# A gMLP's output projection by seven block products instead of eight, with its last column group in another order and the next norm's sums of squares finished by token halves

## The chip, the cores and the metric

The kernel runs on one core of one Trainium2 chip. The metric is the device time of one execution in microseconds (us), as the median of the runs of a kernel. The core's engines appear in the profile as PE (TensorE, matmuls), PEld (its weight loads), DVE (VectorE), ACT (ScalarE), POOL (GpSimd) and SP (SyncE, which here only issues transfers). "SPq", "POOLq" and "ACTq" are the queues through which an engine issues its DMA transfers.

## The reference

The kernel computes a causal decoder trunk of two layers over 512 tokens and 1024 channels in float32. This case concerns the first half of layer 0:

```
def mixer_a(xn, w_in, g_v, w_s, b_s, w_out):
    z = jax.nn.gelu(xn @ w_in)
    u, v = jnp.split(z, 2, axis=-1)
    v = rmsnorm(v, g_v)
    ...
    s = jnp.einsum('hts,bcshd->bcthd', w, v) + b_s.T.astype(v.dtype)[None, None, :, :, None]
    s = s.reshape(B, S, A_WIDTH)
    return (u * s) @ w_out
```

Its result is added to the residual stream h. Then comes `conv_ffn(rmsnorm(h, norm_ffn), ...)`: an up projection to 2 x 2816 channels, a causal convolution of width 3, silu(g) * u, and a down projection that is added to h. Then a per-layer embedding is added, `(p_i @ w_in) * gate`, in which `p_i @ w_in` depends on no h. `rmsnorm` divides each token by the root of the mean of its 1024 squares.

## The kernel before, in words

**Layout.** h lies transposed, as eight tiles h[0] to h[7] of 128 channels by 512 tokens, so a matmul's moving operand has up to 512 columns of tokens. Float32 products are made of three: every operand is split into a high part (the cast `wh`, `ush`, `usl` and so on: a high part ends in h, a low part in l) and the rest, and `mm3` (matmuls at L228) multiplies high by high, high by low and low by high into one accumulator bank of PSUM. A projection from 1024 to 1024 channels is therefore eight output tiles of 8 x 3 = 24 matmuls of 512 columns, 192 in all.

**Weights.** All weights are a list of pieces in order of use (`plan_cols`, `plan_woven`, L63 to L128). SP loads each piece into one of three staging buffers (`load`, L166), ACT casts the high parts (L196), DVE subtracts to get the low parts (L197). A piece is split in units of up to 1024 columns; four units may be ahead of use (`WBUFS`). The instructions of an engine keep the order in which they are scheduled; `behind(x, y)` only says that x shall come after y.

**Seven block products.** The first two of three parts of the FFN's down projection already use `woven_add`. It takes a pair of contraction tiles, a pair of output tiles and the two token halves `first` and `second` as a 2 x 2 by 2 x 2 product of blocks and forms it with seven block multiplications instead of eight, at the price of sums: three sums of weight blocks per piece on DVE (`weave`, L156 to L158) and sums and differences of activations (class `Pair`, L468 to L480). A product is 4 pairs x 3 = 12 matmuls of 256 columns, so a group of 256 output channels takes 84, and the four groups 336. The numbers 1 to 7 name the products. Products 1, 6, 7 and 4 accumulate one after another in half a bank called `dx`; between them that half is copied out (L531, L537, L511), since the partial sums go to different outputs. Products 2, 5 and 3 go into the bank `dy`. The copies, `head`, `rest`, `side` and `tail`, are added to h by accumulating DMA transfers on POOL's queue (L508). Product 4 of a group is run in the next one (`close`), and in the last group product 7 comes before 3, in the others 3 before 7.

**The projection and its surroundings.** In the gating stage (L792 to L818) u is made in four chunks of two tiles: 48 matmuls, then for each tile the gelu and 8 small matmuls of the position mixing (L805), and DVE forms u * s and its splits. Then `dense_add` makes the output projection: after each tile's 24 matmuls (bank `d`) DVE adds the bank to h[m] (L445), ACT squares it (L331), and the squares are added up in `nf0acc` (L336), on POOL for all but the last, which DVE adds. Two small transposes (`turned`, L825) follow, and their copy by DVE (L826).

**The norm.** DVE transposes the sum in blocks of 32 and reduces them (L350, L352, `nf0quarter`); a small matmul `nf0ms` (L361) finishes the mean; DVE adds epsilon (`nf0m`, L426), POOL raises it to the power -1/2 (`nf0rt`, L428), DVE makes an operand of it (`nf0hl`, L381 and L382; `nf0d`, L390), and a matmul `nf0sp` (L394) spreads the factors over all partitions, so that DVE can scale h (L404) for the up projection. PE meanwhile does the embedding's input projection, eight banks of 6 matmuls `pin` (L628 on): `nf0ms` stands after the third bank and `nf0sp` after the sixth. After the eighth, `up` begins (L570).

Of the kernel before, what the change touches and what calls it, by code (L numbers as in the profile page):

```python
# [13 lines left out]
P = 128  # L14
D = 1024
S = 512
# [34 lines left out]
def tile_yoco(ctx: ExitStack, tc: tile.TileContext, t, out: bass.AP, out_b: bass.AP):  # L51
# [64 lines left out]
    plan_cols(t["w_out"], 4, KD)  # L116
# [17 lines left out]
    state = {"raw": 0, "unit": 0, "next": 0, "tags": [0, 1, 2], "turn": 4, "pt": 0, "sent": {}}  # L134
# [82 lines left out]
    def mm3(ps, parts, xs, c0, n=P, first=True, last=True, lows_last=False, onto=False):  # L217
# [9 lines left out]
        for j, (w, x) in enumerate(todo):  # L227
            nc.tensor.matmul(ps, w, x, start=first and j == 0, stop=last and j == len(todo) - 1,  # L228
                             skip_group_check=onto)
# [87 lines left out]
    class Norm:  # L317
# [22 lines left out]
        def take(self, k):  # L340
            if not self.late:
                self.split(k, 0)
            self.square(k, nc.vector if k == KD - 1 else None)
            if self.behind is not None:
                self.behind(k)

# [73 lines left out]
    def inv_root(ms, name, scale=1.0, n=None):  # L420
# [4 lines left out]
        for some, x in ms:  # L425
            nc.vector.tensor_scalar(m[some, :], x, scale, EPS, op0=ALU.mult, op1=ALU.add)  # L426
        r = const.tile([P, n], F32, tag=f"rt{n}", bufs=2, name=f"{name}rt")
        nc.gpsimd.tensor_tensor(r, m, minus_half[:, :n], op=ALU.pow)  # L428
        return r

# [28 lines left out]
    class Pair:  # L459


        def __init__(self, p, edge, name):
            self.p, self.name = p, name
            self.edge = edge[:, p, 0, :], edge[:, p, 1, :]

        def begin(self, a):
            self.a = a
            self.own, self.ones, self.twos = (couple(homes[3 * self.p + x], f"{self.name}_{x}") for x in range(3))  # L468
# [23 lines left out]
    def woven_add(pairs, between):  # L492
# [9 lines left out]
        def product(x, ps, w, at0, first=True):  # L502
            wh, wl = w[:2]
            mm3(ps, [(wh, wl, at0 + k * P) for k in range(len(pairs))], ops[x], 0, first=first,
                onto=not first)
# [7 lines left out]
        def close(c, chain, w, tail):  # L513
            def run():
                product(4, chain, w, 0, first=False)
                minus(tail[:, first], chain)
                onto(h[2 * c + 1], tail)
            return run

        late = None  # L520
        for c in range(4):
            top, low = h[2 * c], h[2 * c + 1]
            chain, other = psum(f"dx{c}")[:, first], psum(f"dy{c}")
            head = tp.tile([P, S], F32, tag="acc", name=f"head{c}")
            tail = tp.tile([P, S], F32, tag="sq", name=f"tail{c}")
            side = tp.tile([P, N], F32, tag="c1", name=f"side{c}")
            rest = tp.tile([P, S], F32, tag="c0", name=f"rest{c}")
            w = unit()
            product(1, chain, w, 0)
            product(2, other[:, first], w, n)  # L530
            nc.scalar.copy(head[:, first], chain)  # L531
            w = unit()
            product(5, other[:, second], w, n)
            product(6, chain, w, 0, first=False)
            minus(side, other[:, second])
            onto(low[:, second], side)
            nc.scalar.copy(head[:, second], chain)  # L537
            onto(top, head)
# [3 lines left out]
            for x in (7, 3) if c == 3 else (3, 7):  # L542
                if x == 3:
                    product(3, other[:, second], w, n, first=False)
                else:
                    product(7, chain, w, 0, first=False)
                    minus(tail[:, second], chain)
            nc.scalar.copy(rest, other)
            onto(top, rest)
            late = close(c, chain, unit(), tail)  # L550
            if c == 0:
                between()
# [848 lines left out]
```

## Time and profile before

Three runs took 1118.29, 1118.88 and 1119.21 us, a median of 1118.88. The profiled execution took 1118.13 us, with a span of 1116.3 us from its first to its last instruction.

| | before |
|---|---|
| gating stage, from its last chunk's matmuls to the projection | 87.57 to 100.25 us |
| output projection, 192 matmuls | 100.25 to 143.79 us |
| `nf0ms`, the norm's mean | 148.19 us |
| `nf0sp`, the norm's factors spread | 152.76 us |
| first matmuls of `up` in the chain | 155.78 us |
| a woven part of the FFN, 336 matmuls | 253.71 to 294.11 us |

All times inside an execution count from the start of the span. In a row of the chain the columns are the start, the duration and the work, with a count. In a row of a timeline they are the start, the duration from the first to the last of a run of like instructions, engine, line, operation and tiles, and in brackets how long the engine was idle before and what released it. In a row of the grouped view, line, engine, operation, tiles, shapes and count stand before the first bar; then the busy time in us and the mean of one in ns; then the idle time before. Tile names come without their numbers.

### The profile page before, as it was taken

How to read it: one execution, taken by the hardware profiler on the slowest of the kernel's cores; microseconds unless marked ns; L12 is line 12 of the kernel's file. 1: busy time of each engine (PE TensorE's matmuls, PEld its weight loads, DVE VectorE, ACT ScalarE, POOL GpSimd, SP SyncE). 2: the span in 40 equal slices, each digit the busy share in tenths (PEclk: the TensorE clock that was granted, in tenths of full speed). 3: DMA queues.
4: the chain of work that ended last, by engine and by line, in shares of the span. 5: the costliest groups of instructions: out<-in, count | busy, mean ns of one | idle time of the engine just before them, and what ended most of it. 6: DMA issues, size and time to landing. Idle time of an engine off the chain costs nothing.

```text
span 1116.3 us, 15052 instructions
## 1 busy us (share of the span) xinstructions
PE 1107.6 (99%) x5693; PEld 947.3 (85%) x5693; DVE 793.8 (71%) x1244; ACT 580.8 (52%) x968; POOL 158.0 (14%) x227
## 2 busy tenths in 40 slices
PE   9999999999999999999999999999999999999997
PEld 7888888889988898888888888888899889988886
DVE  5566368687477675567988997877784777655796
ACT  5733255445544464455656775554464545544543
POOL 1200210002200030012204452000022000300210
PEclk9999999999999999999999999999999999999999
DMA  8632334216931287233134225632179222971333
GB/s 295 137 114 95 113 114 151 76 38 153 244 114 41 84 195 258 84 114 113 54 98 132 77 57 178 213 118 76 38 174 235 101 73 55 226 250 57 114 100 90
DMA packets 46921, 140.95 MB, mean 126 GB/s; under 512 B 12984, under 2 KB 20672, under 8 KB 36352
## 3 DMA queue, kind: packets, MB, share of 16 engines
q1 hardware_dynamic: 35952, 120.38, 33.6%
q0 software_dynamic: 9328, 14.95, 7.6%
q10 hardware_dynamic: 1568, 4.65, 1.1%
q8 instruction: 45, 0.74, 0.3%
q14 instruction: 28, 0.23, 0.1%
HBM read 112.69 MB, written 6.30 MB: 107 GB/s over the span
## 4 chain that ended last, share of the span: by engine, by line
PE 96%; DVE 1%; issue 1%; ACT 1%; POOLq 0%; POOL 0%; DVEq 0%
PE up L228 41%; PE d L228 9%; PE dx L228 8%; PE dy L228 6%; PE o L228 4%; PE q L228 4%; PE gate L228 4%; PE u L228 4%; PE up L570 2%; PE pv L1093 1%; PE v L238 1%; PE v L239 1%; PE v L240 1%; PE pin L228 1%; PE k L228 1%
## 5 line engine op out<-in xcount | busy, mean ns | idle before, releaser
L197 DVE TENSOR_TENSOR wl<-wraw,wh 128x1024 fp32r<-128x1024 f32 (+2 forms) x198 | 232.4, 1179 | 169.6 <-ACT wh L196 168.6
L196 ACT CAST wh<-wraw 128x1024 fp32r<-128x1024 f32 (+2 forms) x197 | 193.7, 990 | 147.1 <-PE up L228 60.6
L582 DVE SCALAR_TENSOR_TENSOR c<-up,vec,c 128x510 f32<-128x510 f32 (+1 forms) x176 | 130.9, 747 | 31.6 <-ACT c L580 29.3
L228 PE MATMUL up<-nf00h,wh 128*128 128x512 f32 x336 | 130.7, 389 | 0.0
L228 PE MATMUL up<-nf10h,wh 128*128 128x512 f32 x336 | 130.7, 389 | 0.0
L228 PE MATMUL up<-nf00l,wh 128*128 128x512 f32 x336 | 130.7, 389 | 0.0
L228 PE MATMUL up<-nf10l,wh 128*128 128x512 f32 x336 | 130.7, 389 | 0.0
L228 PE MATMUL up<-nf10h,wl 128*128 128x512 f32 x336 | 130.5, 389 | 0.0
L228 PE MATMUL up<-nf00h,wl 128*128 128x512 f32 x336 | 130.4, 389 | 0.0
L580 ACT ACTIVATE c<-up,vec 128x512 f32<-128x512 f32 x88 | 68.1, 776 | 44.2 <-PE up L228 39.0
L228 PEld LDWEIGHTS up<-nf00h,wl 128*128 128x128 f32 x336 | 63.1, 188 | 13.2
L228 PEld LDWEIGHTS up<-nf10h,wh 128*128 128x128 f32 x336 | 63.1, 188 | 13.2
L228 PEld LDWEIGHTS up<-nf10h,wl 128*128 128x128 f32 x336 | 63.1, 188 | 13.1
L228 PEld LDWEIGHTS up<-nf00h,wh 128*128 128x128 f32 x336 | 63.1, 188 | 13.0
L228 PEld LDWEIGHTS up<-nf00l,wh 128*128 128x128 f32 x336 | 63.1, 188 | 13.0
L228 PEld LDWEIGHTS up<-nf10l,wh 128*128 128x128 f32 x336 | 63.1, 188 | 12.9
L508 POOL DMA_DIRECT2D h<-side x16 | 14.0, 874 | 403.8 <-ACT side L511 403.8
L197 DVE TENSOR_TENSOR wl<-wsum,wh 128x1024 fp32r<-128x1024 f32 x32 | 39.1, 1223 | 28.5 <-ACT wh L196 28.5
L588 ACT ACTIVATE a<-c 128x512 f32<-128x512 f32 x44 | 27.7, 630 | 39.9 <-DVE c L582 39.9
L196 ACT CAST wh<-wsum 128x1024 fp32r<-128x1024 f32 x32 | 33.6, 1051 | 18.4 <-PE up L228 10.0
L1037 ACT ACTIVATE prs<-prs,neg 128x129 f32<-128x129 f32 x64 | 25.3, 397 | 13.4 <-DVE neg L1032 12.5
L445 DVE TENSOR_TENSOR h<-h,d 128x512 f32<-128x512 f32 x24 | 16.4, 682 | 21.5 <-PE d L228 21.5
(537 smaller groups left out, 2702.7 us busy)
## 6 DMA issues: line engine op xcount, KB each, us to landing
wraw<-in_w_up SPq DMA_DIRECT2D x44, 1024.0 KB, 4.9
wraw<-in_w_down SPq DMA_DIRECT2D x16, 1024.0 KB, 4.9
wraw<-in_w_gate SPq DMA_DIRECT2D x8, 1024.0 KB, 5.0
wraw<-in_w_down SPq DMA_DIRECT2D x8, 768.0 KB, 4.2
wraw<-in_w_u SPq DMA_DIRECT2D x4, 1024.0 KB, 10.2
wraw<-in_w_out SPq DMA_DIRECT2D x4, 1024.0 KB, 4.8
h<-head POOLq DMA_DIRECT2D x16, 256.0 KB, 4.8
h<-rest POOLq DMA_DIRECT2D x16, 256.0 KB, 7.8
```

The lines of the kernel that those rows point to most:

```text
L196: cast = nc.scalar.copy(hi, src)
L197: state["split"] = splits[u] = cast, nc.vector.tensor_sub(low, src, hi.bitcast(F32))
L228: nc.tensor.matmul(ps, w, x, start=first and j == 0, stop=last and j == len(todo) - 1, skip_group_check=onto)
L238: nc.tensor.matmul(ps, xh[:, s], wh[:, a:b], start=st, stop=False)
L239: nc.tensor.matmul(ps, xl[:, s], wh[:, a:b], start=False, stop=False)
L445: nc.vector.tensor_add(h[m], h[m], ps)
L508: nc.gpsimd.dma_start(x, y, accum_op=ALU.add)
L570: nc.tensor.matmul(ps, w[:, off + s * P : off + (s + 1) * P], x, start=k == 0 and x is xh and w is wh, stop=k == KD - 1 and x is xl)
L580: nc.scalar.activation(c, ps, AF.Identity, bias=v("conv_b", l * 2 * NJ + col), scale=cw[2])
L582: ins = nc.vector.scalar_tensor_tensor(c[:, tap:], ps[:, : S - tap], cw[2 - tap], c[:, tap:], op0=ALU.mult, op1=ALU.add)
L588: nc.scalar.activation(a, cs[0], AF.Silu)
L1037: ins = nc.scalar.activation(pr[:, e, :], pr[:, e, :], AF.Exp, bias=neg[:, e : e + 1], scale=-1.0, accum_out=sm[:, e : e + 1])
```

## The change

The output projection's weights are planned as woven, four pieces of four units (1024, 1024, 1024 and 512 columns). The gating stage hands over four `Pair`s instead of eight split tiles; each chunk's two tiles are a pair. For the last chunk the order of the splits is different (`soon`): the difference of the token halves of its first tile is split at once, and its second tile's own split comes first of all. `dense_add` is replaced by `woven_add(us, norm=nf, ...)`, which differs from the FFN's use of it in these points:

- In the first group, products 1, 2 and 5 are run for three pairs, then for the last pair.
- The first two groups add to h by accumulating transfers, as in the FFN, but the last two by additions and subtractions on DVE (`direct`).
- The last group (`ends`) is written out: products 1 and 2, then 4 of the group before, 5, 6, 7, 4 and 3. The scheduler puts `turned` between 6 and 7, and three `pin` between 7 and 4. Fifteen `pin` follow before `nf0ms`, which stays behind the third bank.
- The squares of h[0] to h[5] are summed whole (four adds on POOL, the fifth on DVE). Those of h[6] and h[7] are added, transposed and reduced by token halves on DVE (`by_halves`).
- The copy `turned` and the splits of the first two units of `up` are placed behind `nf0m` on DVE, ahead of `nf0hl`.

In every norm, `take` now gives the last two adds of squares to DVE instead of the last one. In the FFN's woven parts the last group now runs product 3 before 7, as the other groups do.

```diff
-    plan_cols(t["w_out"], 4, KD)
+    plan_woven(t["w_out"], 4, 0, KD)
...
-    state = {"raw": 0, "unit": 0, "next": 0, "tags": [0, 1, 2], "turn": 4, "pt": 0, "sent": {}}
+    state = {"raw": 0, "unit": 0, "next": 0, "tags": [0, 1, 2], "turn": 6, "pt": 0, "sent": {}}
...
-            self.square(k, nc.vector if k == KD - 1 else None)
+            ins = self.square(k, eng or (nc.vector if k >= KD - 2 else None))
...
+        def by_halves(self):
+
+            sqs, a = {}, self.acc
+            sq = tp.tile([P, S], F32, tag="sg", name=f"{self.name}turn")
+            self.quarter = const.tile([P, S // 32], F32, tag="quarter", bufs=1, name=f"{self.name}quarter")
+
+            def add(k, cols):
+                if k not in sqs:
+                    sqs[k] = tp.tile([P, S], F32, tag="sq", name=f"{self.name}sq{k}")
+                ins = nc.scalar.activation(sqs[k][:, cols], h[k][:, cols], AF.Square)
+                return ins, nc.vector.tensor_add(a[:, cols], a[:, cols], sqs[k][:, cols])
+
+            def turn(cols):
+                ins = nc.vector.transpose(sq[:, cols], a[:, cols])
+                return ins, nc.vector.tensor_reduce(self.quarter[:, cols.start // 32 : cols.stop // 32],
+                                                    sq[:, cols].rearrange("p (b f) -> p b f", f=32),
+                                                    axis=mybir.AxisListType.X, op=ALU.add)
+            return add, turn
...
-        def begin(self, a):
+        def begin(self, a, soon=False):
...
+            if soon:
+                split(self.t[:, first], *(x[:, first] for x in self.ones))
...
-        def end(self, b):
+        def end(self, b, soon=False):
             t, u = self.t, tp.tile([P, S], F32, tag="sq", name=f"{self.name}u")
+            if soon:
+                split(b, *self.own)
...
+            if soon:
+                split(u, *self.twos)
+                split(t[:, second], *(x[:, second] for x in self.ones))
+                return
...
-    def woven_add(pairs, between):
+    def woven_add(pairs, between=None, norm=None, tags=("acc", "sq", "c1", "c0")):
...
+                if direct(c):
+                    nc.scalar.copy(tail[:, first], chain)
+                    nc.vector.tensor_sub(h[2 * c + 1], h[2 * c + 1], tail)
+                else:
+                    minus(tail[:, first], chain)
+                    onto(h[2 * c + 1], tail)
...
+        def direct(c):
+            return norm is not None and c > 1
...
+        def ends(c, top, low, chain, other, head, tail):
+
+            w = unit()
+            product(1, chain, w, 0)
+            product(2, other[:, first], w, n)
+            ins = nc.scalar.copy(head[:, first], chain)
+            for m in (2 * c - 2, 2 * c - 3):
+                ins = square(m, ins)
+            late()
+            square(2 * c - 1, None, nc.vector)
+            add, turn = norm.by_halves()
+            w = unit()
+            product(5, other[:, second], w, n)
+            product(6, chain, w, 0, first=False)
+            nc.vector.tensor_sub(low[:, second], low[:, second], other[:, second])
+            nc.vector.tensor_add(top[:, first], top[:, first], other[:, first])
+            nc.scalar.copy(head[:, second], chain)
+            nc.vector.tensor_add(top, top, head)
+            add(2 * c, first)
+            w = unit()
+            product(7, chain, w, 0, first=False)
+            nc.scalar.copy(tail[:, second], chain)
+            nc.vector.tensor_sub(low[:, second], low[:, second], tail[:, second])
+            add(2 * c + 1, second)
+            ends = product(4, chain, unit(), 0, first=False)
+            behind(product(3, other[:, second], w, n, first=False)[0], ends[-1])
+            nc.scalar.copy(tail[:, first], chain)
+            nc.vector.tensor_sub(low[:, first], low[:, first], tail[:, first])
+            seq = [add(2 * c + 1, first)[1]]
+            seq.append(nc.vector.tensor_add(top[:, second], top[:, second], other[:, second]))
+            seq += turn(first)
+            box["sq"], ins = add(2 * c, second)
+            seq += [ins, *turn(second)]
...
+            i = state["next"] + 2
+            behind(splits[i][0], box["sq"])
+            behind(splits[i][1], box["quarter"])
...
+            if c == 0 and norm is not None:
+                w2 = unit()
+                for some in (slice(-1), slice(-1, None)):
+                    product(1, chain, w, 0, first=some.stop is not None, some=some)
+                    if some.stop is None:
+                        nc.scalar.copy(head[:, first], chain)
+                    product(2, other[:, first], w, n, first=some.stop is not None, some=some)
+                    product(5, other[:, second], w2, n, first=False, some=some)
+                w = w2
...
-            for x in (7, 3) if c == 3 else (3, 7):
...
+            product(3, other[:, second], w, n, first=False)
+            product(7, chain, w, 0, first=False)
+            (nc.scalar.copy if direct(c) else minus)(tail[:, second], chain)
+            if direct(c):
+                nc.vector.tensor_add(top, top, head)
+                nc.vector.tensor_add(top, top, other)
+            else:
+                nc.scalar.copy(rest, other)
+                onto(top, rest)
...
+            if norm is not None and c > 1:
+                for m in range(2 * c - 1):
+                    square(m, mark)
...
                     if (c, q, j) == (0, 1, 0):
                         norm.begin(rows=0)
+                        behind(box.pop("turned"), box["m"])
+                        for i in (0, 1):
+                            cast, low = splits[state["next"] + i]
+                            behind(cast, box["sq"])
+                            behind(low, box["m" if i else "quarter"])
...
-            hi = ap.tile([P, S], F32R, tag=f"ah{m}", name=f"ush{m}")
-            lo = ap.tile([P, S], F32R, tag=f"al{m}", name=f"usl{m}")
-            split(u, hi, lo)
-            us.append((hi, lo))
+            (us[c].end if j else us[c].begin)(u, soon=c == 3)
     nf = Norm("nf0", [(xp, "x", gain("norm_ffn", 0))], late=True)
-    dense_add(us, KD, nf)
+    woven_add(us, norm=nf, tags=("c0", "c1", "hs", "sg"))
```

More of the change, by code (lines that the diff above doesn't have):

```diff
@@ L500, in unit, with product @@
             return take()
-        def product(x, ps, w, at0, first=True):
+        def product(x, ps, w, at0, first=True, some=slice(None)):
             wh, wl = w[:2]
-            mm3(ps, [(wh, wl, at0 + k * P) for k in range(len(pairs))], ops[x], 0, first=first,
-                onto=not first)
+            return mm3(ps, [(wh, wl, at0 + k * P) for k in range(len(pairs))][some], ops[x][some], 0,
+                       first=first, onto=not first)
         def onto(x, y):
@@ L541, in woven_add @@
                 late()
-            for x in (7, 3) if c == 3 else (3, 7):
[L543 to L549, printed above, removed]
+            product(3, other[:, second], w, n, first=False)
+            product(7, chain, w, 0, first=False)
+            (nc.scalar.copy if direct(c) else minus)(tail[:, second], chain)
+            if direct(c):
+                nc.vector.tensor_add(top, top, head)
+                nc.vector.tensor_add(top, top, other)
+            else:
+                nc.scalar.copy(rest, other)
+                onto(top, rest)
             late = close(c, chain, unit(), tail)
-            if c == 0:
+            if c == 0 and between:
                 between()
+            if norm is not None and c > 1:
+                for m in range(2 * c - 1):
+                    square(m, mark)
         late()
```

66 lines of the change are left out of this document (39 added, 27 removed).

## The prediction

> **What bounds the kernel now.** I read the page first, then the chain that ended last in order of time around the output projection, then the grouped rows of the stage that already works as the projection is to work, and last the timelines of the engines at the projection's two ends.
>
> ```profile
> span 1116.3 us, 15052 instructions
> PE 1107.6 (99%) x5693; PEld 947.3 (85%) x5693; DVE 793.8 (71%) x1244; ACT 580.8 (52%) x968; POOL 158.0 (14%) x227
> ...
> PE 96%; DVE 1%; issue 1%; ACT 1%; POOLq 0%; POOL 0%; DVEq 0%
> ```
>
> TensorE (PE) carries 96% of the chain. A matmul fewer is worth its pitch, and any wait that reaches PE costs its full length.
>
> ```profile
> 100.25 43.53 PE d L228 x192
> 143.79 0.22 PE turned L825 x2
> 144.01 4.19 PE pin L228 x18
> 148.19 0.29 PE nf0ms L361 x2
> 148.49 4.28 PE pin L228 x18
> 152.76 0.23 PE nf0sp L394
> ```
>
> The projection is 192 matmuls of 512 columns with no gap, 43.53/192 = 0.2267 us each. The norm after it is hidden under `pin`, work that needs no norm: 18 `pin` before `nf0ms`, 18 before `nf0sp`.
>
> ```profile
> 253.71 1.40 PE dx L228 x12
> ...
> 291.23 1.44 PE dy L228 x12
> 292.67 1.44 PE dx L228 x12
> 294.11 5.92 PE up L228 x26
> ```
>
> These are the first and last rows of the chain of an FFN down projection already done with seven block products: four groups of 7 x 12 = 336 matmuls of 256 columns, from 253.71 to 294.11, 40.40 us or 0.1202 us each. The chain names no wait between them.
>
> **The change, part by part.** *Arithmetic.* 192 matmuls of 512 columns become 336 of 256. By the two stretches that is 43.53 - 40.40 = 3.13 us less. The FFN's stretch also has the same weight sums and the same accumulating transfers beside it, so I take -3.13, and it is the ceiling of the gain: all that follows only takes from it. On the pitch the row stands at 0.120 us. [...]
>
> *Weight sums and operand splits.* Four pieces of weights are summed on VectorE (DVE), and each gets four splits instead of two, one of them half as long.
>
> ```profile
> L156 DVE TENSOR_TENSOR wsum<-wraw 128x1024 f32<-128x1024 f32 x8 | 9.8, 1220 | 0.1
> L157 DVE TENSOR_TENSOR wsum<-wsum,wraw 128x512 f32<-128x512 f32 x8 | 5.5, 688 | 0.2
> ...
> L480 DVE SCALAR_TENSOR_TENSOR act_0u<-act_0u,a 128x256 f32<-128x256 f32 x2 | 0.8, 420 | 0.0
> ...
> L531 ACT COPY head<-dx 128x256 f32<-128x256 f32 x8 | 3.0, 373 | 3.1 <-PE dx L228 3.1
> ...
> 60.00:98.50 38.50, 38.50 (x196) 32.77 (x196) 23.91 (x31) 14.70 (x20) 0.00 (x0) 1.00 0.24 83
> ...
> 100.00:143.80 43.80, 43.80 (x198) 36.18 (x196) 18.92 (x22) 14.11 (x18) 8.99 (x6) 1.00 0.32 108
> ...
> 253.60:294.20 40.60, 40.60 (x339) 40.45 (x338) 27.68 (x31) 24.67 (x42) 12.22 (x14) 1.00 0.80 194
> ```
>
> A sum is 1.22 and twice 0.69 (its third operation has the second's form), 2.6 us per piece. The last three rows are windows (sum, then busy PE, weight load, DVE, ACT, POOL): the projection has DVE busy 18.9 of 43.8 us, the FFN's woven stage 27.7 of 40.6. The sums therefore fit beside PE at no cost. Without that cover, a first sum that came late would cost up to its 2.6. The operands lie in the gating stage before: per pair three differences and one edge of about 0.42, and splits for one tile's width more (0.65), 2.3 us in all. That stage's three chunks leave DVE 38.5 - 23.9 = 14.6 us idle, 4.9 each, so the first three pairs cost nothing, with the first sum beside them; only the last pair's stand against PE.
>
> *The start.* The last gating pair is ready late.
>
> ```profile
> 98.51 0.69 DVE L800 TENSOR_TENSOR uz<-u,n0rstd 128x512 f32<-128x512 f32 x1 [0.64 <-PE u L228]
> 99.36 1.23 DVE L197 TENSOR_TENSOR wl<-wraw,wh 128x1024 fp32r<-128x1024 f32 x1 [0.16 <-ACT wh L196]
> 100.50 1.40 DVE L808 SCALAR_TENSOR_TENSOR s<-s,vec,bS 128x512 f32<-128x512 f32 x2
> 101.82 1.28 DVE L811 TENSOR_TENSOR u<-u,s 128x512 f32<-128x512 f32 x2
> 103.19 1.29 DVE L306 TENSOR_TENSOR usl<-u,ush 128x512 fp32r<-128x512 f32 x2
> ...
> 100.01 0.48 PE L228 MATMUL d<-ush,wh 128*128 128x512 f32 x1
> ```
>
> Before, the order of contraction hid this: the last pair's splits end at 104.48 and PE started at 100.01 on the first seven. After, products 1, 2 and 5 of the first three pairs are run first: 27 matmuls, 27 x 0.1202 = 3.2 us, and three of the edge tile (0.36) take PE to about 103.6. The own low half, behind the chain above with the two differences (0.42 each) put in and a weight split halved, is done at about 104.0: a wait of 0.3. Product 7 of this group accumulates onto what the copy of `head` must have read first (0.37); I put 0.2 on that and on product 6's operand. Start: +0.5, with 0 and 1.0 as bounds (the difference of two chains of 4 to 5 us, each good to half a microsecond).
>
> *The end group.* Before, each tile was one DVE add behind its matmuls. In the last group products 6 and 7 use the same half bank, with only `turned` (0.22) between. PE's records last 0.39 and start 0.23 apart, so about 0.16 of drain and the copy of 0.37 must pass, with hand-over some 0.6: less 0.1 to 0.2 of cover, +0.5. Product 4 waits for the copy after 7, under three `pin` (0.70): covered by less than 0.1. Both copies stand in ScalarE's (ACT) list behind squares, and these behind POOL's adds, whose buffers they reuse.
>
> ```profile
> 112.62 1.80 POOL L336 TENSOR_TENSOR nf0acc<-nf0sq,nf0sq 128x512 f32<-128x512 f32 x1 [56.84 <-ACT nf0sq L331]
> ...
> 118.12 1.29 POOL L336 TENSOR_TENSOR nf0acc<-nf0acc,nf0sq 128x512 f32<-128x512 f32 x1 [3.70 <-ACT nf0sq L331]
> ...
> 491.13 1.48 DVE L197 TENSOR_TENSOR wl<-wraw,wh 128x768 fp32r<-128x768 f32 x1 [0.49 <-ACT wh L196]
> ...
> 484.97 0.96 DVE L197 TENSOR_TENSOR wl<-wraw,wh 128x768 fp32r<-128x768 f32 x1
> ```
>
> POOL's add takes 1.29 us alone and 1.80 when a DVE subtraction of two tiles runs over it; DVE's took 1.48 beside POOL against 0.96. Before, the adds were spread over the whole projection. Now four follow one another in the last third, beside adds into h on DVE, each 0.3 to 0.5 longer. I put 0.5 of that on PE (at the copies before 7 and 4), bounds 0 and 1.1. End group: +1.0.
>
> *The norm.* By halves, the chain from product 4's end is copy 0.6, subtraction, square, add and the other tile's add at about 0.42 each, then transpose and reduction of a half twice (0.75 each) with an add between: 4.2 us, against product 3 and fifteen `pin`, 1.44 + 3.5 = 4.9. So `nf0ms` is in time by 0.7. Behind it:
>
> ```profile
> 148.53 0.69 DVE L426 TENSOR_SCALAR nf0m<-nf0ms 32x8 f32<-32x8 f32 x4 [0.49 <-PE nf0ms L361]
> ...
> 149.29 1.65 POOL L428 TENSOR_TENSOR nf0rt<-nf0m,minus_half 128x8 f32<-128x8 f32 x1 [8.06 <-DVE nf0m L426]
> ...
> 150.97 0.17 DVE L381 CAST nf0hl<-nf0rt 128x8 fp32r<-128x8 f32 x1 [1.76 <-POOL nf0rt L428]
> ...
> 151.38 0.69 DVE L390 TENSOR_TENSOR nf0d<-pick,nf0hl 128x512 fp32r<-128x512 f32 x1
> ...
> 152.60 0.39 PE L394 MATMUL nf0sp<-nf0d,ones 128*128 128x512 f32 x1
> ```
>
> `nf0d` ends at 152.07, 0.53 ahead of `nf0sp`. DVE was idle for 1.76 behind `nf0m`, while POOL took the power. Now the copy `turned` and two weight splits (1.23 each) stand there: `nf0hl` starts not 2.44 but 0.69 + 0.3 + 2.4 = 3.4 after `nf0m` began. That is 0.95 later, of which 0.53 is free: +0.4 on PE, which cannot pass `nf0sp`. Bounds 0 and 0.5; I take 0.3.
>
> ```profile
> L196 ACT CAST wh<-wsum 128x1024 fp32r<-128x1024 f32 x32 | 33.6, 1051 | 18.4 <-PE up L228 10.0
> ```
>
> *Everything else.* SP's list holds the same four loads of w_out, with later waits for buffers; the four FFN stages show that two buffers per piece suffice. Their last groups change from product 7, 3 to 3, 7, so that product 4 waits for the copy (0.16 + 0.37) behind three `up` (0.68): nothing, or, if ACT is then inside a 1.05 cast, up to 0.6 in each of four places. In the other norms one POOL add becomes a DVE add, off PE's path.
>
> Sum: -3.13 + 0.5 + 1.0 + 0.3 = -1.3. The profiled execution took 1118.13 us (span 1116.3 and 1.83 around it); it would take about 1116.8. The runs' median, 1118.88, is 0.75 above it and gives 1117.5. Differences under 0.2% (2.24 us) are about what a measurement of this kernel can't tell from no change.
>
> **The rivals.** *All hidden.* The copies and POOL's adds fit, and only the 0.5 of products 6 and 7 remains, or half of it: -2.3 to -2.9, 1116.3. For it: the FFN's woven stages show no gap at 336 matmuls. Against it: there no group is last before a norm, and product 7 had cover.
>
> *The power locks the port.* If POOL's 1.65 us power shuts out DVE's weight split as the adds shut out each other, the two splits start only when it ends and `nf0hl` is 1.4 later still: -1.3 + 1.4 = +0.1, 1119.0. For it: 491.13 against 484.97. Against: the power reads only 8 elements per partition, and no row shows a DVE operation of two inputs beside it. [...]
>
> *A transfer comes late: slower.* Before, no h tile of the norm went through DMA; now h0 to h3 do.
>
> ```profile
> h<-rest POOLq DMA_DIRECT2D x16, 256.0 KB, 7.8
> h<-tail POOLq DMA_DIRECT2D x16, 256.0 KB, 7.3
> ...
> wraw<-in_w_up SPq DMA_DIRECT2D x1, 1024.0 KB, 9.5
> ...
> h<-tail POOLq DMA_DIRECT2D x1, 256.0 KB, 9.1
> ```
>
> The first two are the medians, the last two one stretch where a transfer ran beside a 1 MB load. The last one of h3 is issued about 0.6 after product 4 of the second group. Its square, POOL's add (1.3 to 1.8) and DVE's add of the sixth square must be through when product 6 of the last group is copied, 84 matmuls or 10.1 us after that product 4: free up to a landing of about 6.6 us, and from there 1 us for 1 us, less what the norm's 0.7 covers. A landing at 9.1 costs 2.5: +1.2, 1120.1. It decides from about 7.9 us on (a cost of 1.3), and passes the 0.2% only near 10.2, or with the port's lock. For it: the medians 7.8 and 7.3; a load of w_up starts at about that time. Against: in the projection DMA is busy 0.32 of the time, not 0.80 as in the FFN.
>
> **How the numbers follow.** Forecast 0.46 (-0.4 to -2.1), all hidden 0.27, lock 0.11, late transfer 0.16. The forecast and the lock lie within 0.2%, but for 0.03 of the lock with other costs added; all hidden is faster; of the late transfer 0.13 is slower by over 0.2%, when more than one transfer is late or the lock adds to it. Faster 0.27, same 0.57, slower 0.16. The range runs from 1115.9 (-3.0, nearly the ceiling) to 1120.6 (+1.7, a landing near 9.5).
>
> **What would show it.** Right: 336 `dx`, `dy` matmuls, in about 40.4 us plus waits; a gap of about 0.3 before the last pair's matmuls; about 0.5 to 1.0 before the last product 7; `nf0ms` without a wait and `nf0sp` 0.3 late; POOL's adds at 1.3 to 1.8. Wrong: a pitch over 0.125; a chain with `h` DMA in it; `nf0rt` with no DVE split beside it; gaps at product 4 of the FFN's last groups; waits at the first weights of a piece, which would say that the sums do not fit.

## The result, and the profile after

The changed kernel took 1120.12 us (median of 22 runs, 1119.3 to 1122.22) against 1118.49 before (22 runs, 1117.56 to 1119.63): a ratio of 1.0018, 95% interval 1.0012 to 1.0025. It is slower by 1.6 us by the medians and 2.0 by the ratio; the forecast was 1.3 faster (1117.5). The columns of all rows are those explained ahead of the prediction. The profiled execution took 1120.09 us. The page's first lines, answering to those shown of before:

```profile
span 1118.3 us, 15472 instructions
...
PE 1105.6 (99%) x5837; PEld 951.4 (85%) x5837; DVE 822.4 (74%) x1300; ACT 597.3 (53%) x1007; POOL 161.0 (14%) x230
...
PE 95%; DVE 1%; issue 1%; ACT 1%; DMA 1%; POOL 0%; POOLq 0%
```

PE is busy 2.0 us less, and the span is 2.0 longer: PE waits. Around the projection, PE's timeline names three waits in brackets:

```profile
138.05 0.38 PE L227 MATMUL dx<-us_1h,wh 128*128 128x256 f32 x1 [0.43 <-ACT head L578]
...
140.70 0.96 PE L227 MATMUL pin<-own_m,wh 128*128 128x512 f32 x3 [0.95 <-ACT wh L196]
...
154.53 0.47 PE L413 MATMUL nf0sp<-nf0d,ones 128*128 128x512 f32 x1 [2.15 <-DVE nf0d L409]
```

The first is the last product 7, which the prediction had. The second stands before the first `pin`, whose weights came late; the chain in order of time shows why:

```profile
133.53 0.67 DVE h L645
134.21 1.11 DVE wl L197
135.32 0.02 issue
135.34 4.24 DMA wraw<-in_w_pin
139.57 0.02 issue
139.60 1.05 ACT wh L196
140.65 0.04 issue
140.70 0.96 PE pin L227 x3
```

The chain runs from the split of w_out's last unit (`wl`) over the load and the cast to `pin`. The load of 512 KB is issued only at 135.34, when the split of w_out's last unit has given back the last of the staging buffers, and lands 4.24 us later. The third wait is the norm's. POOL's power and DVE beside it:

```profile
149.09 4.16 POOL L447 TENSOR_TENSOR nf0rt<-nf0m,minus_half 128x8 f32<-128x8 f32 x1 [10.94 <-DVE nf0m L445]
```

```profile
149.04 0.41 DVE L931 COPY turned<-turned 8x256 f32<-8x256 f32 x1
149.38 2.34 DVE L197 TENSOR_TENSOR wl<-wraw,wh 128x1024 fp32r<-128x1024 f32 x2
153.29 0.17 DVE L400 CAST nf0hl<-nf0rt 128x8 fp32r<-128x8 f32 x1 [1.56 <-POOL nf0rt L447]
```

The power lasts 4.16 us, 1.65 before. The two weight splits on DVE are not longer for it (2.34 for two; 2.35 in a run below in which POOL stands idle beside them), and the power ends 1.53 after them.

For the balance I count each matmul's start from the projection's first matmul, which takes out what happens earlier (start, first matmul: 100.01 before, 100.58 changed). The gating stage's last `u` matmul started at 97.94 to 98.75 in six profiles of kernels with the old projection and at 97.78 to 98.74 in eleven with the new one; of the 1.96 us between the two profiles 0.57 is a difference of this kind, which lies within that spread and isn't counted as the change's. From `up` to the end both take 960.7, so no cost shows in the FFN's reordered groups.

| us from the projection's first matmul | before | changed |
|---|---|---|
| `turned` | 43.62 | 36.66 |
| last product 7 | - | 37.47 |
| first `pin` | 43.75 | 40.12 |
| `nf0ms` | 48.08 | 47.26 |
| `nf0sp` | 52.59 | 53.95 |
| `up` | 55.61 | 57.03 |

So the change cost 1.42 us there: the 3.13 of arithmetic were gained, and 4.55 lost again.

### The profile page after: what moved, and what is told of

Read it like the earlier page. It is cut to its first block, busy times and chain, and to the rows that moved or that the text cites. A ratio compares the mean times of both kernels' runs of the same rounds, so it can differ in the third digit from the quotient of the medians.

```text
span 1118.3 us, 15472 instructions
## 1 busy us (share of the span) xinstructions
PE 1105.6 (99%) x5837; PEld 951.4 (85%) x5837; DVE 822.4 (74%) x1300; ACT 597.3 (53%) x1007; POOL 161.0 (14%) x230
## 4 chain that ended last, share of the span: by engine, by line
PE 95%; DVE 1%; issue 1%; ACT 1%; DMA 1%; POOL 0%; POOLq 0%
PE up L227 41%; PE dx L227 10%; PE dy L227 7%; PE d L227 6%; PE q L227 4%; PE gate L227 4%; PE u L227 4%; PE o L227 3%; PE up L672 2%; PE v L239 1%; PE gt L237 1%; PE v L237 1%; PE gt L239 1%; PE v L238 1%; PE gt L238 1%; PE k L227 1%
## 5 line engine op out<-in xcount | busy, mean ns | idle before, releaser
L197 DVE TENSOR_TENSOR wl<-wraw,wh 128x1024 fp32r<-128x1024 f32 (+2 forms) x198 | 229.4, 1164 | 146.9 <-ACT wh L196 146.0
L197 DVE TENSOR_TENSOR wl<-wsum,wh 128x1024 fp32r<-128x1024 f32 x40 | 49.6, 1240 | 33.8 <-ACT wh L196 33.8
L196 ACT CAST wh<-wsum 128x1024 fp32r<-128x1024 f32 x40 | 42.0, 1051 | 21.6 <-PE up L227 10.0
L691 DVE TENSOR_TENSOR a<-a,c 128x512 f32<-128x512 f32 x44 | 30.4, 691 | 1.7 <-ACT a L690 0.2
```

The source lines that it names most:

```text
L196: cast = nc.scalar.copy(hi, src)
L197: state["split"] = splits[u] = cast, nc.vector.tensor_sub(low, src, hi.bitcast(F32))
L691: nc.vector.tensor_mul(a, a, cs[1])
```

## The experiments

**The norm's factor.** First the order alone was changed in the changed kernel:

```diff
+                for i in (0, 1):
+                    behind(splits[u + i][1], self.d)
```

> The changed kernel with one order changed on DVE: `nf0hl` and `nf0d` come before the two weight splits of `up`, not behind them. In the changed kernel's trace the power `nf0rt` lasts 4.16 us (1.65 before) and PE waits 2.15 us at `nf0sp`. Theory A, POOL's power is shut out while DVE subtracts two tiles: without a split beside it `nf0rt` is back at about 1.65, the wait at `nf0sp` is gone, and the time falls by about 2.0 us against the changed kernel (the splits may cost up to 0.5 later, in front of `nf0x`): about 1118.1, level with before. Rival B, the power is long for a reason of its own and only the queue on DVE counts: `nf0rt` stays near 4.2, `nf0hl` can't start earlier, and the time falls by less than 0.3 us.

It took 1118.16 us (11 runs, 1117.26 to 1118.47), ratio to before 0.9995 (0.9986 to 1.0004). The power and DVE's list in it:

```profile
148.91 1.67 POOL L450 TENSOR_TENSOR nf0rt<-nf0m,minus_half 128x8 f32<-128x8 f32 x1 [10.96 <-DVE nf0m L448]
```

```profile
148.86 0.41 DVE L934 COPY turned<-turned 8x256 f32<-8x256 f32 x1
150.61 0.17 DVE L400 CAST nf0hl<-nf0rt 128x8 fp32r<-128x8 f32 x1 [1.33 <-POOL nf0rt L450]
...
151.63 2.35 DVE L197 TENSOR_TENSOR wl<-wraw,wh 128x1024 fp32r<-128x1024 f32 x2
```

The power is back at 1.67, the wait at `nf0sp` is gone, and `up` starts at 55.23 instead of 57.03; 0.28 returns as a wait before `up`. Theory A holds: the splits beside the power were worth 1.8 us of the region (the stretch from the projection's first matmul to `up`), and 2.0 of the time by the medians.

Then, to see what in the splits holds POOL up, subtractions were put beside the power of the kernel before, first four short ones:

```diff
+            for i in range(4):
+                x = tp.tile([P, S], F32, tag="hs", name=f"probe{i}")
+                ins = nc.vector.tensor_sub(x, h[2 * i], h[2 * i + 1])
+                behind(ins, last)
+                last = ins
```

> The kernel before, with four DVE subtractions of two 128x512 tiles of h (results unused, about 0.69 us each, 2.76 in all) put between `nf0m` and `nf0hl`. Theory A (a DVE operation with two tiles of input shuts POOL out): `nf0rt` lasts 1.65 + about 2.5 = 4.0 to 4.4 us, `nf0hl` waits for it, and PE waits about 2.0 us at `nf0sp`. Rival B (only DVE's own queue counts): `nf0rt` stays at 1.65, `nf0hl` starts behind the four, 0.5 to 0.6 us later than before, of which most is covered: a wait of 0.1 to 0.7 at `nf0sp`.

```profile
149.74 2.15 POOL L430 TENSOR_TENSOR nf0rt<-nf0m,minus_half 128x8 f32<-128x8 f32 x1 [8.05 <-DVE nf0m L428]
```

Neither: 2.15 us, not 4.0, though DVE subtracted for 2.51. Two long ones were tried next, the second after the first on one tile, and then on tiles of their own (the edit shown):

```diff
+            for i in range(2):
+                x = mp.tile([P, D], F32R, tag=f"m{3 - i}", name=f"probe{i}")
+                ins = nc.vector.tensor_sub(x, hi.bitcast(F32), lo.bitcast(F32))
```

> The kernel before, with two DVE subtractions of 128x1024 elements that write fp32r, like weight splits (results unused), between `nf0m` and `nf0hl`. Four subtractions of 512 columns in this place made `nf0rt` 2.15 us long, not the 4.0 expected. Theory A1 (POOL gets the port only between two DVE instructions, and these two leave it no opening): `nf0rt` is 3.5 to 4.3 us long as in the changed kernel, PE waits 1.5 to 2.1 us at `nf0sp`. Theory A2 (the long power of the changed kernel has a further cause beside the two splits, such as the casts and transfers of that moment): `nf0rt` stays at 1.7 to 2.3 us and the wait is under 0.4.

> As the run with two long subtractions in the kernel before, but each writes a tile of its own, so that the second need not wait for the first. There `nf0rt` lasted 2.69 us: POOL seems to have got through when the first subtraction ended (it ended 1.12 us after the power began, and 1.12 + 1.57 = 2.69). Theory A1 (without a wait between them, the two hold POOL out together, as in the changed kernel): `nf0rt` is 3.7 to 4.2 us. Theory A3 (POOL always gets in between two DVE instructions): 2.6 to 2.8 us as before, and the long power of the changed kernel needs another cause.

The power took 2.69 us in the first and 2.68 in the second, whose rows are:

```profile
149.19 2.68 POOL L430 TENSOR_TENSOR nf0rt<-nf0m,minus_half 128x8 f32<-128x8 f32 x1 [8.06 <-DVE nf0m L428]
```

```profile
149.14 2.37 DVE L436 TENSOR_TENSOR probe<-own_m,own_m 128x1024 fp32r<-128x1024 f32 x2
```

The power begins 0.05 after the first subtraction and ends 1.5 after that one's end (149.14 + 2.37/2 = 150.33), although the second runs on. A wait between the two is not what lets POOL in, so A1 fell for this arrangement. In the changed kernel, the copy was moved between the splits:

```diff
-                        behind(box.pop("turned"), box["m"])
+                        behind(splits[state["next"] + 1][1], box["m"])
+                        behind(box["turned"], splits[state["next"] + 1][1])
+                        behind(splits[state["next"] + 2][1], box.pop("turned"))
```

> The changed kernel with the small copy `turned` (it reads PSUM, 0.41 us) moved from ahead of the two splits of `up` to between them. Theory A1 (POOL needs an opening between two subtractions): the power gets through after the first split, `nf0rt` is 2.6 to 3.1 us, the wait at `nf0sp` falls from 2.15 to 0.9 to 1.3 us. Theory A3 (the number of splits between `nf0m` and `nf0hl` counts, not the opening): `nf0rt` stays at 4.0 to 4.3 us.

The power took 2.70, the wait at `nf0sp` was 0.68, the run 1118.46. A1 foresaw that power too, but after the run before it is no sign for A1: again the power begins 0.05 after a split and is through 1.5 after its end. What the slow case has of its own is that the power begins first, beside the copy, and the split 0.29 later. That order was then built into the kernel before, the copy and two free subtractions:

```diff
+            behind(tcopy, last)
+            last = tcopy
```

> The kernel before with the copy `turned` and then two free subtractions of 128x1024 between `nf0m` and `nf0hl`: the order of the changed kernel. Theory A4 (a power that has begun before a subtraction and is caught by it is held to the end of the whole row of subtractions): `nf0rt` is 3.9 to 4.3 us, PE waits 1.7 to 2.2 us at `nf0sp`. Theory A3 (it gets in at the end of the first subtraction): `nf0rt` is 2.8 to 3.2 us and the wait 0.7 to 1.1 us; then something else of the changed kernel holds it.

```profile
149.10 4.14 POOL L430 TENSOR_TENSOR nf0rt<-nf0m,minus_half 128x8 f32<-128x8 f32 x1 [8.00 <-DVE nf0m L428]
```

```profile
149.05 0.41 DVE L842 COPY turned<-turned 8x256 f32<-8x256 f32 x1
149.39 2.34 DVE L438 TENSOR_TENSOR probe<-own_m,own_m 128x1024 fp32r<-128x1024 f32 x2
```

4.14 us and a wait of 1.97 at `nf0sp`: the changed kernel's case, in the kernel before. So a power that began 0.3 us before two subtractions, beside the copy, ended 1.5 us after both (4.14 and 4.16 us long); one that began 0.05 behind a subtraction ended 1.5 after that one, though another followed (2.68 to 2.70). The changed kernel shows the second case once more, in layer 1's first norm, where a split now stands beside the power (1.65 before, 2.69 now; PE doesn't wait there):

```profile
567.07 2.69 POOL L447 TENSOR_TENSOR n1rt<-n1m,minus_half 128x8 f32<-128x8 f32 x1 [16.07 <-DVE n1m L445]
```

```profile
567.02 1.23 DVE L197 TENSOR_TENSOR wl<-wraw,wh 128x1024 fp32r<-128x1024 f32 x1
```

That this is so is shown; why is not. Every power of over 4 us also had the copy ahead of the subtractions; the copy alone does nothing (1.67 above), but a run with the 0.3 us and without the copy was not made. Nor is the order of the starts enough to tell which engine's row grows. With a subtraction first POOL's row did (2.68), and not that of the second subtraction, which began while the power ran (2.37 for the two in the row above). In the slow case POOL was first, by the profile's starts, and again its own row grew (4.14 to 4.16) and not the two of DVE (2.34).

**The first `pin`.** The buffers of the two pieces were exchanged, alone and together with the norm's order:

```diff
+        if name == f"wraw{pins}":
+            i, j = state["turn"] % 3, (state["turn"] + 1) % 3
...
+            tags[i], tags[j] = tags[j], tags[i]
```

> The changed kernel with the staging buffers of the two `pin` pieces exchanged, so that the first of them is loaded into the buffer that comes free first (133.6 in the changed kernel's trace) and not into the one that comes free last (135.3). Theory A, the wait of 0.95 us before the first `pin` is the late load alone: it is gone, and the time falls by 0.9 to 1.1 us against the changed kernel, to about 1119.0. Rival B, the cast on ACT or the DMA's own time decides (two loads at once land later): more than 0.4 us of the wait stays.

> Both edits at once. If the two waits are independent, as both stand on PE's path one behind the other, the gains add: about -3.0 us against the changed kernel, 1117.1, some 1.3 us faster than the kernel before. If the earlier `pin` only lets PE arrive sooner at a norm that is not ready (the last half's reduction ended 0.56 before `nf0ms` began), half of the second gain is lost at `nf0ms`: -2.5 us.

1120.36 us (1119.96 to 1122.33), ratio 1.0022 (1.0013 to 1.0031), and 1118.36 (1117.85 to 1118.96), ratio 0.9998 (0.9989 to 1.0007): the exchange gained nothing in either. PE's row of the first of them says why:

```profile
138.31 0.73 PE L233 MATMUL pin<-own_m,wh 128*128 128x512 f32 x2 [0.96 <-ACT wh L202]
```

The load did land earlier: ACT's cast behind it, 1.05 us long, was through when `pin` began at 138.31, so it ran from 137.26 at the latest, instead of from 139.60. But the scheduler, seeing `pin` ready sooner, had put two of them ahead of product 7, and the cast ahead of the copy of `head`. The wait moved forward with them; the one at `nf0sp` was 2.40 in the first run. With that order held fixed, and then with the second split of `up` put behind the second `nf0x`:

```diff
+                        behind(mms[0], box.pop("seven"))
+                        behind(box.pop("four"), mms[2])
...
+            behind(splits[i - 1][0], copied)
```

> The kernel with both edits, and the order held that the scheduler had changed there: the first `pin` stay behind product 7 and ahead of product 4, and the cast of their weights on ACT stays behind the second copy of `head`. Theory A (the late load is all that PE waits for at the first `pin`): the load is issued at 133.5 and lands near 137.5, the cast is done near 139.2, before PE comes there, so the wait of 0.95 us is gone, and the time is 0.8 to 1.1 us under that of the kernel with only the norm's order changed (1118.2): about 1117.2, 0.12% under before. Rival B (ACT's list, not the load, decides, since the cast now stands behind the copy): a wait of 0.4 or more stays at `pin` or at product 4, and the gain is under 0.5 us.

```diff
+                if k == 1 and self.name == "nf0":
+                    behind(splits[u + 1][1], ins)
```

> As the run before, and the second of the two weight splits of `up` is put behind the second `nf0x` instead of ahead of the first. With only the norm's order changed PE waited 0.28 us before the first `up`. If that wait comes from `nf0x` standing behind both splits, it goes: another -0.2 to -0.3 us, about 1117.0. If DVE is then late with the low halves for the fifth tile instead, the gain is 0 or a loss of up to 0.3.

1117.54 us (1117.21 to 1118.44), ratio 0.9993 (0.9984 to 1.0002), and 1117.42 (1117.12 to 1117.89), ratio 0.9989 (0.9981 to 0.9998). The wait for the high half is gone; another one remains in both (the first's row):

```profile
140.47 0.50 PE L233 MATMUL pin<-own_m,wl 128*128 128x512 f32 x1 [0.52 <-DVE wl L203]
```

So the gain foreseen for the first (0.8 to 1.1 us) did not come in full: the load was the first cause, as theory A said, but behind it stood DVE's list with the split of the low halves, which neither theory named. By the starts `up` came at 55.12 in the first and at 54.48 in the second, against 55.23 with the norm's order alone. In the last step of this series, `pin` that need low halves were put behind product 3:

```diff
+                        behind(mms[2], box["three"])
+                    elif "four" in box:
+                        behind(box.pop("four"), mms[1])
+                        behind(mms[2], box["three"])
```

> The kernel with the second split later, and the first `pin` that need the low halves of their weights put behind product 3; four that need the high halves alone stand between products 7 and 4. There PE waited 0.52 us for the low halves' split, which comes behind the adds into h on DVE. If the remaining wait at `pin` is only that, it goes: -0.5 to -0.7 us, about 1116.8, 0.16% under before. If PE then arrives at `nf0ms` before the norm, part of it comes back there, and the gain is under 0.3.

1117.37 us (1116.45 to 1117.58), ratio 0.9988 (0.9979 to 0.9996). PE has no wait at `pin` any more, and `up` starts at 53.96 instead of 54.48, so 0.5 us was gained in the region; the medians show 0.05, and the intervals of the two ratios overlap almost wholly.

**POOL's adds.** With all these waits mended, the four adds of squares were given to DVE; then the same in the changed kernel alone, and in it with the norm's order:

```diff
-                ins = square(m, ins)
+                ins = square(m, ins, nc.vector)
...
-                    square(m, mark)
+                    square(m, mark, nc.vector)
```

> The run below (norm's order, buffer and `pin` mended) with the four adds of squares of POOL given to DVE. The prediction put 0.5 us of POOL's adds on PE, at the copies before products 7 and 4. If that is so, the wait before the last product 7 (0.50 to 0.62) falls to 0.2 to 0.3 and the time by 0.3 to 0.5 us. If the wait is only the drain and the copy, it stays at 0.5, and the time is within 0.2 us of the run below.

> The changed kernel with nothing but the four adds of squares given to DVE. If POOL's adds cost it time on PE at the copies and at the late split of the fourth unit (DVE's subtractions beside them took 1.91 and 1.18 us against 1.22 and 0.6), the buffer for the first `pin` comes free about 1.2 us earlier and most of the wait of 0.95 goes too: -1.0 to -1.3 us, about 1118.9. If they matter only once the other waits are mended: within 0.3 us of the changed kernel's 1120.1.

> Two edits only: the norm's `nf0hl` and `nf0d` ahead of the two splits, and the four adds on DVE; the buffers and the order of `pin` as in the changed kernel. If the late `pin` load is itself a consequence of POOL's adds, this is as fast as the version with all edits (1115.9): 1115.8 to 1116.4. If the load needs the other buffer, 0.6 to 1.0 slower than that: 1116.5 to 1117.0.

| | median us (range) | ratio to before | `up` from the projection's first matmul |
|---|---|---|---|
| changed | 1120.12 (1119.3 to 1122.22) | 1.0018 (1.0012 to 1.0025) | 57.03 |
| adds on DVE alone | 1120.62 (1119.21 to 1121.28) | 1.0016 (1.0007 to 1.0025) | 58.84 |
| norm's order | 1118.16 (1117.26 to 1118.47) | 0.9995 (0.9986 to 1.0004) | 55.23 |
| norm's order, adds on DVE | 1117.31 (1116.8 to 1118.06) | 0.9991 (0.9982 to 1.0) | 55.24 |
| norm's order, `pin` mended | 1117.37 (1116.45 to 1117.58) | 0.9988 (0.9979 to 0.9996) | 53.96 |
| the same, adds on DVE | 1115.88 (1115.41 to 1116.26) | 0.9974 (0.9964 to 0.9983) | 53.37 |

The 58.84 of the second row holds a fall of the clock of about 1.6 us, which is read below; the kernel before has 55.61.

Beside POOL's adds DVE is slower in the changed kernel, and faster without them, as these rows show of the changed kernel and of the fastest one:

```profile
131.70 1.91 DVE L197 TENSOR_TENSOR wl<-wsum,wh 128x1024 fp32r<-128x1024 f32 x1 [0.33 <-ACT wh L196]
...
134.13 1.18 DVE L197 TENSOR_TENSOR wl<-wraw,wh 128x512 fp32r<-128x512 f32 x1
135.76 1.25 DVE L547 TENSOR_TENSOR h<-h,tail 128x512 f32<-128x512 f32 x1 [0.45 <-ACT tail L546]
```

```profile
132.41 1.22 DVE L203 TENSOR_TENSOR wl<-wsum,wh 128x1024 fp32r<-128x1024 f32 x1
...
134.15 0.69 DVE L203 TENSOR_TENSOR wl<-wraw,wh 128x512 fp32r<-128x512 f32 x1
...
135.62 0.69 DVE L558 TENSOR_TENSOR h<-h,tail 128x512 f32<-128x512 f32 x1 [0.18 <-ACT tail L557]
```

But while `pin` waits for its load, that is worth nothing: the region is the same with and without (55.23 and 55.24), since the load lands no earlier. With the adds on DVE it is issued 0.35 us sooner, counted from the projection's first matmul (100.16 here, 100.58 in the changed kernel), but it takes 4.89 instead of 4.24, by its row in the chain:

```profile
134.57 4.89 DMA wraw<-in_w_pin
```

So here the late load is not the adds' doing; why the transfer took longer is not shown. With `pin` mended the adds are worth 0.6 us by the region and 1.5 by the medians. The times of the two kernels don't overlap, so the gain is real; the traces explain 0.6 of it, and the rest is open. The fastest version is 0.26% faster than the kernel before (0.17 to 0.36%). There the wait before the last product 7 is 0.24, from 0.42 with the adds on POOL.

**The clock after the wait.** The changed kernel's 22 runs form two groups: twelve from 1119.3 to 1120.13 with a mean granted clock of 0.998 or 0.999, and ten from 1120.96 to 1122.22 with 0.996 or 0.997. To see whether the wait does that, seven subtractions were put into the kernel before, which make PE wait and nothing else:

```diff
+            for i in range(7):
+                x = tp.tile([P, S], F32, tag="hs", name=f"probe{i}")
+                ins = nc.vector.tensor_sub(x, h[i % 4], h[i % 4 + 4])
```

> The kernel before, with seven subtractions of 512 columns between `nf0m` and `nf0hl` (results unused, 7 x 0.63 = 4.4 us), so that PE idles about 2.0 to 2.3 us at `nf0sp` and nothing else changes. The runs of the changed kernel lie in two groups, 13 of 22 near 1119.8 and 9 from 1121.0 to 1122.2, with mean clocks of 0.998 to 0.999 and 0.996 to 0.997; without the wait at `nf0sp` the runs form one group. Theory C (an idle time of that length on PE makes the clock give way in some executions): two groups here too, about 1120.7 and 1122.3, the later ones at the lower clock. Rival D (the two groups come from another part of the change): one group near 1120.7 at 0.998.

The wait at `nf0sp` was 1.97. The 11 runs went from 1120.17 to 1122.11, median 1121.29, ratio 1.0023 (1.0015 to 1.0032): six from 1120.17 to 1121.29 at 0.998 or 0.999, and of the five from 1121.66 on, four at 0.996 or 0.997. Theory C holds. The run with the buffers alone exchanged, whose wait was 2.40, shows the same: 6 of its 11 are at 0.996 or 0.997. The profiled execution of the changed kernel with its adds on DVE happened to be at such a clock, and shows the place. Windows (their sum, then busy PE, PEld, DVE, ACT, POOL, then the granted clock, DMA share, GB/s):

```profile
148.00:152.00 4.00, 4.00 (x18) 3.10 (x17) 3.49 (x8) 3.73 (x7) 3.06 (x1) 1.00 0.61 180
152.00:154.00 2.00, 0.23 (x1) 0.00 (x0) 0.80 (x3) 0.58 (x1) 1.10 (x1) 1.00 0.83 281
154.00:156.00 2.00, 1.62 (x5) 1.33 (x6) 1.32 (x3) 0.32 (x1) 0.00 (x0) 0.67 1.06 438
156.00:158.00 2.00, 2.00 (x6) 1.61 (x5) 1.97 (x4) 1.46 (x3) 0.00 (x0) 0.50 1.03 432
158.00:160.00 2.00, 2.00 (x10) 1.59 (x9) 1.97 (x4) 1.63 (x4) 0.75 (x2) 0.97 0.83 328
160.00:164.00 4.00, 4.00 (x19) 3.31 (x18) 3.97 (x7) 2.32 (x4) 0.44 (x1) 1.00 0.34 137
```

PE waits 2.15 us at `nf0sp`, and the clock granted after it is 0.67, 0.50 and 0.97 in the three windows from 154, which lack 2 x (0.33 + 0.50 + 0.03) = 1.72 us of full clock. At the 0.50 of the middle window throughout, that is an estimated 1.72/0.50 = 3.4 us. PE starts 6 matmuls in the 2 us from 156 and 10 in those from 158; by its rows the eight `pin` starts from 154.68 on, up to the one at 158.07, are 3.39/8 = 0.42 apart, and those from 158.33 on 0.23. From `nf0sp` to `up` this kernel takes 58.84 - 54.20 = 4.64 us, the changed kernel's profiled execution 57.03 - 53.95 = 3.08: 1.56 us, about the distance of the two groups, whose medians are 1119.83 and 1121.54.

## Why the prediction was wrong

The forecast was -1.3 us, and the region showed +1.42. That 1120.12 lies inside the stated range (1115.9 to 1120.6) is luck: its slow end was reckoned from a late transfer of h, and the time came from two waits that it had put at nothing and at 0.3. Term by term, from the starts in the balance above:

- *Arithmetic, -3.13:* right. The projection's first 300 matmuls are 300 x 0.1202 = 36.06 us of the 36.66 up to `turned`.
- *Weight sums and the accumulating transfers:* right that they cost nothing; no wait of PE between the first and the last group names them. The rival of a late h transfer did not come about: none of PE's three waits is released by one. The transfer that came late was one of weights.
- *The start, +0.5:* 36.66 - 36.06 = 0.60.
- *The end group, +1.0:* the wait before product 7 was 37.47 - 36.66 - 0.22 = 0.59, near the half put there, though 0.2 of it is the adds' (the wait in brackets falls from 0.43 to 0.24 with the adds on DVE). The half for POOL's adds was wrong for this kernel as it stands. DVE was slower by 0.5 to 0.7 for an instruction, where the prediction took 0.3 to 0.5, but with the adds on DVE alone nothing was gained, because `pin` waited longer for its load (1.28 instead of 0.95). With `pin` mended the adds cost 0.6 in the region.
- *Everything else, 0:* this is the first step that failed. The prediction took from the FFN's stages that two buffers per piece suffice. They do within a stage: PE has no wait for weights inside the projection. What it did not follow is the piece after the last one: `pin` takes the buffer of w_out's last piece, and the loads of before (first one issued at 113.30, 30 us ahead of the first `pin`) could no longer be early. By the starts the first `pin` came 40.12 - 37.47 - 12 x 0.1202 = 1.21 us late. The timelines of SP, before and changed:

```profile
113.30 11.21 SPq L166 DMA_DIRECT2D wraw<-in_w_pin  x2
```

```profile
133.64 2.03 SPq L166 DMA_DIRECT2D wraw<-in_w_pin  x2
```

- *The norm, +0.3:* the second step, and the larger one. It took the power at 1.65 us from a row in which DVE was idle, and let only DVE's queue count. It took 4.16, and `nf0sp` came 53.95 - 47.26 - 4.37 = 2.32 late, where 4.37 is the distance of the two with the norm's order changed. That the power and the splits could hold each other up stood among the rivals, as a lock of a port, with 0.11; but it was priced as DVE waiting for POOL (+1.4), while POOL's row grew from 1.65 to 4.16 and DVE's two splits took 2.34, as alone (2.35). No run shows a port, or what it does.

The sum by measured terms is -3.13 + 0.60 + 0.59 + 1.21 + 2.32 = 1.59, against 1.42 in the trace. With both waits mended the region gained 55.61 - 53.96 = 1.65 us, so the gain that was forecast was there to be had, at the price of these two steps. What the 22 runs show beyond that (1.63 by the medians, 2.0 by the ratio) fits the clock's drop in 10 of them, which the prediction did not know.

## What to carry to other kernels

When work is moved beside an operation whose duration comes from a row, look at what the other engines did in that row: a duration measured beside an idle engine was too short here (1.65 for what became 4.16), and both directions of a contention need a price. When a stage takes more staging buffers, follow the loads of the stage after it, and count from when the last buffer comes free. A mended wait is worth its length only when nothing stands right behind it: here the adds on DVE were worth nothing until `pin` was ready (`up` at 55.23 and 55.24, then 53.96 and 53.37), and an earlier load nothing until the scheduler's own reordering was held (medians 1120.36 against 1120.12, then 1117.54 against 1118.16).

## What the runs showed of the hardware that was not expected

- POOL's power of 128x8 elements took 1.65 to 1.68 us with no subtraction beside it; 2.15 when it began 0.05 after the first of a row of 512-column DVE subtractions; 2.68 to 2.70 when it began 0.05 after one of 1024 columns, with or without a second behind it; and 4.14 to 4.16 when it began 0.3 before two of these, beside a small copy. In the second and third case it ended 1.5 to 1.6 us after the first subtraction, in the last 1.5 after the second. In the last case DVE took 2.34 us for its two, as without POOL beside them (2.35).
- A wait of PE of 1.97 to 2.40 us was followed by a mean clock of 0.996 or 0.997 in some of the executions (10 of 22 in the changed kernel, 8 of 11 with its adds on DVE, 6 of 11 with the buffers exchanged, 4 of 11 in the one before with the wait built in), and one of 0.998 or 0.999 in the others. In the one trace that shows it the granted clock fell to 0.50 behind the wait, for an estimated 3.4 us (1.72/0.50, above), at a cost of 1.6 us; in the 75 runs of the seven kernels whose waits are all under 1.5 us no mean clock was under 0.998.
